# Stationary tiles with 16 or 32 bytes between their rows, in a two-layer decoder trunk on one core

## The chip, the cores and the metric

The kernel runs on one core of a Trainium2 chip. The metric is the device time of one execution in microseconds (us), lower is better; before the change it is 2203.47 us, the median of two runs (2203.27 to 2203.67).

## What is computed

A trunk of two layers over 256 tokens of width 2048, all in float32. Layer 0 mixes tokens by spatial gating and a sparse attention, layer 1 by a short convolution; both end in a gated feed-forward of width 5632. Cut to what matters here, the products with the large weights:

```python
def trunk(x):                                   # x [256, 2048]
    h = x
    h = h + mixer0(rmsnorm(h) @ w_in_ab) @ w_out_ab    # [2048, 4632], [2048, 2048]
    h = h + swiglu(rmsnorm(h), w_gate[0], w_up[0], w_down[0])
    b, c, z = split(rmsnorm(h) @ w_in_c, 3)             # [2048, 6144]
    h = h + (b * conv3(c * z)) @ w_out_c                # [2048, 2048]
    h = h + swiglu(rmsnorm(h), w_gate[1], w_up[1], w_down[1])
    return rmsnorm(h)

def swiglu(h, w_gate, w_up, w_down):            # [2048, 5632] x2, [5632, 2048]
    return (silu(h @ w_gate) * (h @ w_up)) @ w_down
```

## The kernel before

Every product is computed by the class `Stream`. A weight is read once, in blocks of 512 columns, and a block in loads of four K tiles (128 rows each) into one of three `raw` tiles. Two K tiles are a unit. `split` makes two fp32r parts of a unit's weights: ScalarE writes the high part `wh` (L82), VectorE the rest `wl` (L83). `multiply` then issues, for each K tile and each of the two token tiles, three matmuls that add up in one PSUM bank: high activations by high weights (L99), high by low (L100), low by high (L101). In all of them the activations are the stationary operand, 128 x 128 values that a weight load (LDWEIGHTS in the profile, engine row PEld) puts into the array, and 512 columns of weights are the moving one. `run` keeps the split three units ahead of the products, and calls hooks between units, in which the rest of the work stands (transposes, attention, evictions).

The activations that are stationary are kept as pairs of tiles, high and low, with one row of S = 256 values for each K tile: `a_h` and `a_l` (16 K tiles, the normed input of every first product), `t_h` and `t_l` (44 K tiles, the hidden layer of the feed-forward, source of `w_down`), `z_h` and `z_l` (16, the convolution's result, source of `w_out_c`), and `y0` and `y1` (16, the mixer's result, source of `w_out_ab`; the profile calls both y). They are written by `split_T`: transposes on TensorE into a PSUM bank (L223), then ScalarE writes the high part (L234, L239) and VectorE the low one (L235, L241), two K tiles at once in L234 and L235. y's attention half is written at L615 and L616 instead.

A K tile's row is 256 x 4 = 1024 bytes, and the second token tile starts 512 bytes into it. So every stationary operand of a tile starts at the same place modulo 512 bytes. The moving tiles have rows of 2048 bytes, and their starts also agree modulo 512.

Two more groups of products use fp32r: the gate's (L496, stationary 48 columns from an `xv` tile with rows 192 bytes apart, moving 256 columns of a_h or a_l) and the compressed blocks' (L398, stationary 60 columns from an earlier y tile with rows 240 bytes apart, moving 128 columns of weights).

`rest_loads` (L203) loads gains and encodings into two small constant tiles, `rows` and `pes`, with six DMAs from ScalarE's queue; `rest_T` transposes them (L213, L214). The pool `tok` has two buffers of 4096 bytes a partition, used in turn by tiles called `tk`, among them the two of L379, in which the windows of the compression are built.

Of the kernel before, what the change touches and what calls it, by code (L numbers as in the profile page):

```python
# [8 lines left out]
F32 = mybir.dt.float32  # L9
# [6 lines left out]
P = 128  # L16
S = 256
# [10 lines left out]
NEG = -1e30  # L28
AHEAD = 3
PROBS, VALUES = 4, 6  # L30


class Stream:
    """Weight tiles in the order of their use: loaded, split into two 12-bit parts, multiplied."""

    def __init__(self, nc, raws, parts, psg):
        self.nc, self.raws, self.parts, self.psg = nc, raws, parts, psg
# [4 lines left out]
        self.at_unit = 0  # L42

    def gemm(self, w, groups, n0, src, done, tail=0, between=None):
        """One column block of a product: K tiles in groups of four, or (first, number), two of them a unit. In the last `tail` units the
        first token tile goes before the second. `between` has units to put between the groups."""
        chunk = {"ps": None, "done": done}
        for gi, g in enumerate(groups):
            k0, gk = g if isinstance(g, tuple) else (g, 4)
            ri = len(self.raw_plan)  # L50
            self.raw_plan.append((w[k0 * P:(k0 + gk) * P, n0:n0 + NW].rearrange("(k p) n -> p k n", p=P), gk * NW))
            for j in range(gk // 2):
                self.units.append({
                    "raw": ri, "j": j, "k0": k0 + 2 * j, "src": src, "chunk": chunk, "free": j == gk // 2 - 1,
                    "first": gi == 0 and j == 0, "last": gi == len(groups) - 1 and j == gk // 2 - 1, "tail": 0,
                })
            if between and gi < len(groups) - 1:
                ap, use = between.pop(0)
                self.units.append({"raw": len(self.raw_plan), "j": 0, "use": use, "free": True})
                self.raw_plan.append((ap, 2 * NW))  # L60
        if tail:
            self.units[-tail]["tail"] = tail
# [86 lines left out]
def trunk(ctx: ExitStack, tc: tile.TileContext, x, norm_mix, norm_ffn, norm_f, w_in_ab, w_out_ab, sgu_w, sgu_b,  # L149
# [14 lines left out]

    st = Stream(nc, raws, parts, psg)

    # ---- residual stream, gains, constants
    h = acts.tile([P, MT, D], F32, name="h")
    a_h = acts.tile([P, KT, S], F32R, name="a_h")
    a_l = acts.tile([P, KT, S], F32R, name="a_l")  # L170

    row0 = const.tile([16, P], F32, name="row0")
    rows = const.tile([104, P], F32, name="rows")
    pes = const.tile([64, P], F32, name="pes")
    xt = x[0].rearrange("(m p) d -> p m d", p=P)

    def x_load(eng, c):
# [5 lines left out]
    nc.gpsimd.memset(mhalf, -0.5)  # L183

    def fold(n):
        """[2n, n]: two identities, one below the other"""
        t = const.tile([2 * n, n], F32, name=f"fold{n}")
        nc.gpsimd.memset(t, 0.0)
        for base in (0, -n):
            nc.gpsimd.affine_select(out=t, in_=t, compare_op=ALU.not_equal, fill=1.0, base=base, pattern=[[-1, n]],  # L190
                                    channel_multiplier=1)
        return t
# [8 lines left out]
    g_sgub = gains[:, 112:120]  # L201

    def rest_loads():  # L203
        nc.scalar.dma_start(out=rows[0:16], in_=norm_mix[1].rearrange("(k p) -> k p", p=P))
        nc.scalar.dma_start(out=rows[16:48], in_=norm_ffn.rearrange("l (k p) -> (l k) p", p=P))
        nc.scalar.dma_start(out=rows[48:96], in_=conv_w.rearrange("o j (k p) -> (o j k) p", p=P))
        nc.scalar.dma_start(out=rows[96:104], in_=sgu_b[0])
        nc.scalar.dma_start(out=pes[0:32], in_=cmp_pe_k[0])
        nc.scalar.dma_start(out=pes[32:64], in_=cmp_pe_v[0])

    def rest_T():
        t = bank()
        nc.tensor.transpose(t[:, :104], rows, ident[:104, :104])  # L213
        nc.tensor.transpose(t[:, 104:168], pes, ident[:64, :64])  # L214
        nc.vector.tensor_copy(gains[:, 16:], t[:, :104])
        nc.vector.tensor_copy(peT, t[:, 104:168])

    def transposed_bank(src, c):
        """A bank [P, 2, S]: the transpose of two 128-column tiles of src [P, MT, *] from column c."""
        t = bank()  # L220
        for k in range(2):
            for m in range(MT):
                nc.tensor.transpose(t[:, k * S + m * P:k * S + (m + 1) * P], src[:, m, c + k * P:c + (k + 1) * P], ident)  # L223
        return t.rearrange("p (k s) -> p k s", s=S)
# [21 lines left out]
        nc.scalar.activation(j, src, AF.Square, accum_out=into)  # L246

    def rsqrt_mean(ss, n, width, name, r=None):
        """1 / sqrt(ss / n + eps) of ss [P, width]"""
        v = small.tile([P, width], F32, name="v_" + name)  # L250
        nc.vector.tensor_scalar(v, ss, 1.0 / n, EPS, op0=ALU.mult, op1=ALU.add)
        if r is None:
            r = const.tile([P, width], F32, name="r_" + name)
        nc.gpsimd.tensor_tensor(r, v, mhalf[:, :width], op=ALU.pow)
        return r
# [6 lines left out]
    R = {}  # L262

    def norm_from(name, gain, after=None):
        """A callback for the column blocks of a product that adds to h and feeds the next norm."""
        ssp = const.tile([P, MT, 4], F32, name="ssp_" + name)

        def block(c):
            def done(ps):
                for m in range(MT):  # L270
                    hs = h[:, m, c * NW:(c + 1) * NW]
                    nc.vector.tensor_add(hs, ps[m], hs)
                    square_sum(hs, ssp[:, m, c:c + 1])

                def later():
                    split_T(transposed(h, c * NW), (a_h, a_l), 4 * c, gain)
                    if c == 3:
                        R[name] = row_scale(ssp, name)
                        if after:
                            after()  # L280

                st.at(1, later)

            return done

        return block

    # ---- layer 0: projections, gated spatial mixing, sparse attention
    stage = ExitStack()

    def region(name, bufs=1):
# [22 lines left out]
    def x_tiles(b):  # L314
        split_T([transposed_bank(h, b * S)], (a_h, a_l), 2 * b, g_mix[0])

    # masks and biases of the attention
    NC = 15
    dist, cbias, cmask = [], [], []

# [48 lines left out]
    def done_cmp(ps):  # L369
        x_scale()  # L370
        t = []

        def later(i):
            """The windows of 32 rows, with their encodings, as [d, row, part, group, window]."""
            w = tok.tile([P, MT * NW], F32, name="tk")[:, :64 * NC].rearrange("p (l g c) -> p l g c", l=32, g=2)
            v = transposed_bank(t[0], i * S).rearrange("p g (c l) -> p l g c", l=16)
            for j in range(2):
                pe = peT[:, i * 32 + 16 * j:i * 32 + 16 * j + 16]
                nc.vector.tensor_add(w[:, 16 * j:16 * j + 16], v[:, :, :, j:j + NC],  # L379
                                     pe[:, :, None, None].to_broadcast([P, 16, 2, NC]))  # L380
            xc[i] = yp.tile([P, 32, 2, 2 * NC], F32R, name=f"y{i}")
            w = w.rearrange("p l g c -> p l (g c)")
            nc.scalar.activation(xc[i][:, :, 0], w, AF.Copy)
            nc.vector.tensor_sub(xc[i][:, :, 1], w, xc[i][:, :, 0].bitcast(F32))

        st.at(1, lambda: t.append(to_tok(ps, r0)))
        st.at(2, lambda: later(0))
        st.at(3, lambda: later(1))
# [55 lines left out]
        nc.gpsimd.memset(t, 0.0)  # L444

    def cmp_out_v():
        """The compressed values, once for each head of a group: rows 32 r to 32 r + 14 for head r."""
        t = bank()
        for g in range(2):
            nc.tensor.matmul(t[:, g * P:(g + 1) * P], hgv[:, g].rearrange("p r n -> p (r n)"), w2[:, 1], start=True,  # L450
# [140 lines left out]
        nc.vector.tensor_mul(sm, sm, gv[:, :, 0])  # L591
        nc.vector.tensor_mul(s, s, sm[:, :, None].to_broadcast([P, 4, NC]))
    def compressed_T(g, qt):
        """The transposed probabilities of four heads, as the diagonal blocks of pcT."""
        t = bank()
        nc.tensor.transpose(t[:, :P], csp[(2 * g + qt) % 2].rearrange("p r n -> p (r n)"), ident)
        for r in range(4):
# [18 lines left out]
        nc.vector.tensor_sub(y_l[:, hs, qs], ov, y_h[:, hs, qs].bitcast(F32))  # L616

    def attention(first, step):
        """Background work between the units: each stage some units after the one that it waits for."""
        for g in range(2):  # L620
            for qt in range(MT):
                u = first + step * (8 * g + 4 * qt)
# [112 lines left out]
    for c in range(4):  # L735
        st.gemm(w_out_ab[0], [0, 8, 12, 4], c * NW, src_y, blk(c))

    # ---- feed-forward
    ff = {}

    def feed_forward(layer, rname, blk):
        src = [None, None]

        def done_gate_ff(c):
            def done(ps):
                if c == 0:
                    next_region()
                    big = region(f"big{layer}")
                    ff["tk"] = region(f"fft{layer}")
                    src[0] = big.tile([P, FKT, S], F32R, name="t_h")  # L750
                    src[1] = big.tile([P, FKT, S], F32R, name="t_l")
                t = ff["tk"].tile([P, MT, NW], F32, name="ga")
                for m in range(MT):
                    nc.scalar.activation(t[:, m], ps[m], AF.Silu, scale=R[rname][:, m:m + 1])
# [23 lines left out]

    feed_forward(0, "f0", norm_from("c1", g_mix[1]))

    # ---- layer 1: gated short convolution
    cv = {}
    wc = w_in_c[0]
    src_z = [None, None]
# [1 line left out]
    def done_cg(c):  # L786
        def done(ps):
            if c == 0:
                next_region()
                pool = region("conv")  # L790
                cv["p"] = region("convt", 2)
                src_z[0] = pool.tile([P, KT, S], F32R, name="z_h")
                src_z[1] = pool.tile([P, KT, S], F32R, name="z_l")
                r2 = const.tile([P, MT], F32, name="r2")
                nc.vector.tensor_mul(r2, R["c1"], R["c1"])
                cv["r2"] = r2
# [52 lines left out]
    for c in range(4):  # L849
        st.gemm(w_out_c[0], G4, c * NW, src_z, blk(c))  # L850

    # ---- last feed-forward and norm
    nf = {}
    ssf = const.tile([P, MT, 4], F32, name="ssp_o")

# [55 lines left out]
    g_ps = bank()  # L911

    def keep_warm(n):
        """Transposes of the identity, to nowhere, while the tensor engine has no data yet."""
        for _ in range(n):
            nc.tensor.transpose(g_ps[:, P:2 * P], ident, ident)

# [46 lines left out]
```

## Time and profile before

| what | value |
| --- | --- |
| median of the runs | 2203.47 us |
| span of the profiled execution, first to last instruction | 2201.5 us |
| time around the span (median less span) | 2.0 us |
| TensorE busy, matmul rows | 2190.7 us |
| weight loads (PEld) | 1797.6 us |
| VectorE busy | 1149.7 us |
| ScalarE busy | 988.1 us |
| mean granted TensorE clock | 0.999 |

The profile is of one execution. A matmul's row runs until its last result is out, so rows of matmuls that follow each other overlap, and their mean length is more than the time from one start to the next; the latter is read from the timeline, whose first column is the start and second the length. In the chain of waits, pieces are cut where the next begins, so that `x8` beside 0.94 us is eight steps in that time. Rows of groups give busy time and the mean of one in ns, then the idle time before them.

### The profile page before, as it was taken

The page shows a single profiled execution, that of the slowest core. Times are in us where ns is not written, and L with a number is a line of the kernel's source. Part 1 is how long each engine was busy: PE and PEld are TensorE (multiplying, and loading weights), DVE is VectorE, ACT ScalarE, POOL GpSimd, SP SyncE. Part 2 cuts the span into 40 slices and gives each one's busy share as a digit, 9 for nine tenths or more (in the row PEclk, how much of TensorE's full clock was granted, in tenths as well). Part 3 has the DMA queues.
Part 4 walks back from the last instruction along what each step waited for, and adds up shares of the span by engine and source line. Part 5 has one row for each costly group of instructions (what it writes and reads, how often), then busy time and mean ns, then how long its engine had stood idle before and what let it go on. Part 6 is the DMA issues. An engine that isn't in the chain of part 4 may idle for free.

```text
span 2201.5 us, 24410 instructions
## 1 busy us (share of the span) xinstructions
PE 2190.7 (100%) x9900; PEld 1797.6 (82%) x9900; DVE 1149.7 (52%) x1269; ACT 988.1 (45%) x1178; POOL 28.6 (1%) x59
## 2 busy tenths in 40 slices
PE   9999999999999999999999999999999999999998
PEld 7887788888888888888888888888888888888886
DVE  6577655455445544444455555554544455444444
ACT  6456545444444444444444444444444444434443
POOL 2000000000000000000000000000000000000000
PEclk9999999999999999999999999999999999999999
DMA  8654455656655555555556555556655655555553
GB/s 261 207 190 134 135 184 179 191 191 191 191 191 190 182 190 185 190 188 180 187 186 197 191 184 179 191 188 193 188 188 190 191 191 191 191 187 191 191 189 133
DMA packets 214577, 410.95 MB, mean 187 GB/s; under 512 B 6744, under 2 KB 18448, under 8 KB 214464
## 3 DMA queue, kind: packets, MB, share of 16 engines
q1 hardware_dynamic: 210416, 404.52, 56.7%
q10 hardware_dynamic: 3664, 3.63, 0.5%
q8 instruction: 77, 1.26, 0.2%
q0 software_dynamic: 384, 1.25, 0.2%
q14 instruction: 36, 0.29, 0.0%
HBM read 407.27 MB, written 2.10 MB: 186 GB/s over the span
## 4 chain that ended last, share of the span: by engine, by line
PE 99%; issue 0%; DMA 0%; DVE 0%; SPq 0%; POOLq 0%; POOL 0%; ACT 0%; DVEq 0%
PE pg L99 32%; PE pg L101 32%; PE pg L100 32%; PE pm L223 2%; PE pm L532 0%; PE pm L609 0%; PE pm L398 0%; PE pm L565 0%; DMA h<-in_x_dram 0%; PE pm L496 0%; PE pm L683 0%; PE pm L612 0%; PE pm L572 0%; POOLq L959 0%; POOL nf_r L892 0%
## 5 line engine op out<-in xcount | busy, mean ns | idle before, releaser
L83 DVE TENSOR_TENSOR wl<-raw,wh 128x1024 fp32r<-128x1024 f32 (+1 forms) x769 | 939.3, 1224 | 937.1 <-ACT wh L82 933.4
L82 ACT ACTIVATE wh<-raw 128x1024 fp32r<-128x1024 f32 (+1 forms) x769 | 811.8, 1058 | 976.7 <-PE pg L101 967.2
L99 PE MATMUL pg<-wh,a_h 128*128 128x512 f32 x2080 | 820.2, 394 | 0.0
L101 PE MATMUL pg<-wh,a_l 128*128 128x512 f32 x2080 | 810.4, 390 | 0.0
L100 PE MATMUL pg<-wl,a_h 128*128 128x512 f32 x2080 | 809.9, 389 | 0.0
L99 PEld LDWEIGHTS pg<-wh,a_h 128*128 128x128 f32 x2080 | 390.9, 188 | 81.5 <-issue 2.2
L100 PEld LDWEIGHTS pg<-wl,a_h 128*128 128x128 f32 x2080 | 390.9, 188 | 81.4 <-issue 2.2
L101 PEld LDWEIGHTS pg<-wh,a_l 128*128 128x128 f32 x2080 | 390.6, 188 | 81.8
L99 PE MATMUL pg<-wh,t_h 128*128 128x512 f32 x704 | 278.2, 395 | 0.0
L101 PE MATMUL pg<-wh,t_l 128*128 128x512 f32 x704 | 277.8, 395 | 0.0
L100 PE MATMUL pg<-wl,t_h 128*128 128x512 f32 x704 | 277.8, 395 | 0.0
L99 PEld LDWEIGHTS pg<-wh,t_h 128*128 128x128 f32 x704 | 132.6, 188 | 31.0
L101 PEld LDWEIGHTS pg<-wh,t_l 128*128 128x128 f32 x704 | 132.6, 188 | 31.0
L100 PEld LDWEIGHTS pg<-wl,t_h 128*128 128x128 f32 x704 | 132.6, 188 | 30.8
L99 PE MATMUL pg<-wh,y 128*128 128x512 f32 x128 | 51.0, 398 | 0.0
L99 PE MATMUL pg<-wh,z_h 128*128 128x512 f32 x128 | 50.8, 397 | 0.0
L100 PE MATMUL pg<-wl,z_h 128*128 128x512 f32 x128 | 50.5, 395 | 0.0
L101 PE MATMUL pg<-wh,z_l 128*128 128x512 f32 x128 | 50.5, 395 | 0.0
L101 PE MATMUL pg<-wh,y 128*128 128x512 f32 x128 | 50.4, 394 | 0.0
L100 PE MATMUL pg<-wl,y 128*128 128x512 f32 x128 | 50.4, 394 | 0.0
L235 DVE TENSOR_TENSOR t_l<-pm,t_h 128x512 fp32r<-128x512 f32 x44 | 28.4, 686 | 32.5 <-ACT t_h L234 32.5
L234 ACT ACTIVATE t_h<-pm 128x512 fp32r<-128x512 f32 x44 | 23.9, 597 | 46.3 <-PE pm L223 46.3
(182 smaller groups left out, 780.1 us busy)
## 6 DMA issues: line engine op xcount, KB each, us to landing
raw<-in_w_gate_dram SPq DMA_DIRECT2D x88, 1024.0 KB, 5.1
raw<-in_w_up_dram SPq DMA_DIRECT2D x88, 1024.0 KB, 5.2
raw<-in_w_down_dram SPq DMA_DIRECT2D x88, 1024.0 KB, 5.1
raw<-in_w_in_c_dram SPq DMA_DIRECT2D x48, 1024.0 KB, 5.1
raw<-in_w_in_ab_dram SPq DMA_DIRECT2D x34, 1024.0 KB, 5.2
raw<-in_w_out_ab_dram SPq DMA_DIRECT2D x16, 1024.0 KB, 5.1
raw<-in_w_out_c_dram SPq DMA_DIRECT2D x16, 1024.0 KB, 5.1
raw<-in_w_in_ab_dram SPq DMA_DIRECT2D x4, 512.0 KB, 6.6
```

What stands on the lines that cost most here:

```text
L82: nc.scalar.activation(hv[:, ks], src[:, ks], AF.Copy)
L83: nc.vector.tensor_sub(lv[:, ks], src[:, ks], hv[:, ks].bitcast(F32))
L99: nc.tensor.matmul(ps[m], xh[:, kt, sl], hv[:, k, :], start=u["first"] and k == 0, stop=False)
L100: nc.tensor.matmul(ps[m], xh[:, kt, sl], lv[:, k, :], start=False, stop=False)
L101: nc.tensor.matmul(ps[m], xl[:, kt, sl], hv[:, k, :], start=False, stop=u["last"] and k == 1)
L223: nc.tensor.transpose(t[:, k * S + m * P:k * S + (m + 1) * P], src[:, m, c + k * P:c + (k + 1) * P], ident)
L234: nc.scalar.activation(dh[:, k0:k0 + 2, :], t, AF.Copy)
L235: nc.vector.tensor_sub(dl[:, k0:k0 + 2, :], t, dh[:, k0:k0 + 2, :].bitcast(F32))
```

## The change

The tiles a_h, a_l, z_h and z_l get rows of S + 8 values, t_h and t_l of S + 4, of which the first S are used as before; y keeps its rows. `rows` and `pes` are no longer tiles of their own (512 bytes a partition each), but slices of a `tk` tile. The rest of the diff takes out comments.

```diff
+PAD, FPAD = 8, 4
...
-    a_h = acts.tile([P, KT, S], F32R, name="a_h")
-    a_l = acts.tile([P, KT, S], F32R, name="a_l")
+    a_h = acts.tile([P, KT, S + PAD], F32R, name="a_h")[:, :, :S]
+    a_l = acts.tile([P, KT, S + PAD], F32R, name="a_l")[:, :, :S]
...
-    rows = const.tile([104, P], F32, name="rows")
-    pes = const.tile([64, P], F32, name="pes")
...
     def rest_loads():
+        t = tok.tile([P, MT, NW], F32, name="tk")
+        rows, pes = t[:104, 0, :P], t[:64, 1, :P]
+        rest.extend((rows, pes))
...
+    rest = []
+
     def rest_T():
+        rows, pes = rest
...
-                    src[0] = big.tile([P, FKT, S], F32R, name="t_h")
-                    src[1] = big.tile([P, FKT, S], F32R, name="t_l")
+                    src[0] = big.tile([P, FKT, S + FPAD], F32R, name="t_h")[:, :, :S]
+                    src[1] = big.tile([P, FKT, S + FPAD], F32R, name="t_l")[:, :, :S]
...
-                src_z[0] = pool.tile([P, KT, S], F32R, name="z_h")
-                src_z[1] = pool.tile([P, KT, S], F32R, name="z_l")
+                src_z[0] = pool.tile([P, KT, S + PAD], F32R, name="z_h")[:, :, :S]
+                src_z[1] = pool.tile([P, KT, S + PAD], F32R, name="z_l")[:, :, :S]
```

On each engine the built program has the same instructions in the same order as before; only the shape that L234 and L235 write for t changes, from 128x512 to 128x2x256. The places in the partition, from the memory maps of the two programs (start in bytes, and that modulo 512):

| tile | start before | mod 512 | row before | start after | mod 512 | row after |
| --- | --- | --- | --- | --- | --- | --- |
| wh, first buffer (moving) | 44,672 | 128 | 2048 | 43,648 | 128 | 2048 |
| wl, first buffer (moving) | 61,056 | 128 | 2048 | 60,032 | 128 | 2048 |
| a_h | 93,824 | 128 | 1024 | 92,800 | 128 | 1056 |
| a_l | 110,208 | 128 | 1024 | 109,696 | 128 | 1056 |
| t_h | 129,024 | 0 | 1024 | 129,024 | 0 | 1040 |
| t_l | 174,080 | 0 | 1024 | 174,784 | 192 | 1040 |
| z_h | 129,024 | 0 | 1024 | 129,024 | 0 | 1056 |
| z_l | 145,408 | 0 | 1024 | 145,920 | 0 | 1056 |
| y0 | 163,776 | 448 | 1024 | 163,776 | 448 | 1024 |
| y1 | 180,160 | 448 | 1024 | 180,160 | 448 | 1024 |

## Rows read from the trace of the kernel before

**Rows 1.** The page, part 1: busy us (share of the span) x instructions

```profile
span 2201.5 us, 24410 instructions
PE 2190.7 (100%) x9900; PEld 1797.6 (82%) x9900; DVE 1149.7 (52%) x1269; ACT 988.1 (45%) x1178; POOL 28.6 (1%) x59
```

**Rows 2.** The page, part 4: the chain that ended last, by engine and line

```profile
PE 99%; issue 0%; DMA 0%; DVE 0%; SPq 0%; POOLq 0%; POOL 0%; ACT 0%; DVEq 0%
PE pg L99 32%; PE pg L101 32%; PE pg L100 32%; PE pm L223 2%; PE pm L532 0%; PE pm L609 0%; PE pm L398 0%; PE pm L565 0%; DMA h<-in_x_dram 0%; PE pm L496 0%; PE pm L683 0%; PE pm L612 0%; PE pm L572 0%; POOLq L959 0%; POOL nf_r L892 0%
```

**Rows 3.** Windows by stage (mostly y, a, t, z as stationary operand)

```profile
core 0: us, PE busy (x) PEld busy (x) DVE busy (x) ACT busy (x) POOL busy (x), PEclk, DMA share, GB/s
...
260.00:362.00 102.00, 102.00 (x456) 82.05 (x456) 54.30 (x61) 49.64 (x68) 0.00 (x0) 1.00 0.52 169
362.00:852.00 490.00, 490.00 (x2210) 406.66 (x2209) 246.22 (x226) 214.04 (x226) 1.61 (x1) 1.00 0.59 189
852.00:1101.00 249.00, 249.00 (x1089) 202.00 (x1088) 118.55 (x111) 103.90 (x120) 0.00 (x0) 1.00 0.56 185
...
1365.00:1462.00 97.00, 97.00 (x441) 79.13 (x440) 52.90 (x58) 47.37 (x68) 0.00 (x0) 1.00 0.54 179
1462.00:1951.00 489.00, 489.00 (x2203) 405.75 (x2202) 245.49 (x226) 211.97 (x223) 2.71 (x3) 1.00 0.60 191
```

**Rows 4.** Groups: matmuls of each stationary tile, and a weight load

```profile
L99 PE MATMUL pg<-wh,a_h 128*128 128x512 f32 x2080 | 820.2, 394 | 0.0
...
L99 PEld LDWEIGHTS pg<-wh,a_h 128*128 128x128 f32 x2080 | 390.9, 188 | 81.5 <-issue 2.2
...
L99 PE MATMUL pg<-wh,t_h 128*128 128x512 f32 x704 | 278.2, 395 | 0.0
...
L99 PE MATMUL pg<-wh,y 128*128 128x512 f32 x128 | 51.0, 398 | 0.0
L99 PE MATMUL pg<-wh,z_h 128*128 128x512 f32 x128 | 50.8, 397 | 0.0
```

**Rows 5.** Timeline of TensorE, products with a_h and a_l, 15 rows

```profile
499.69 0.39 PE L99 MATMUL pg<-wh,a_h 128*128 128x512 f32 x1
...
502.87 0.39 PE L101 MATMUL pg<-wh,a_l 128*128 128x512 f32 x1
```

**Rows 6.** Timeline of TensorE, products with y, 12 rows

```profile
349.83 0.39 PE L100 MATMUL pg<-wl,y 128*128 128x512 f32 x1
...
352.40 0.39 PE L99 MATMUL pg<-wh,y 128*128 128x512 f32 x1
```

**Rows 7.** Timeline of TensorE, products with t_h and t_l, 18 rows

```profile
1001.02 0.39 PE L100 MATMUL pg<-wl,t_h 128*128 128x512 f32 x1
...
1003.35 0.40 PE L101 MATMUL pg<-wh,t_l 128*128 128x512 f32 x1
1003.59 0.39 PE L99 MATMUL pg<-wh,t_h 128*128 128x512 f32 x1
...
1004.98 0.40 PE L99 MATMUL pg<-wh,t_h 128*128 128x512 f32 x1
```

**Rows 8.** Timeline of TensorE, products with z_h and z_l, 15 rows

```profile
1419.62 0.40 PE L101 MATMUL pg<-wh,z_l 128*128 128x512 f32 x1
...
1422.88 0.40 PE L100 MATMUL pg<-wl,z_h 128*128 128x512 f32 x1
```

**Rows 9.** The chain of waits in time: gate, compressed blocks, transposes, plain products

```profile
63.82 0.94 PE pm L496 x8
64.76 0.96 PE pm L398 x16
...
145.04 0.87 PE pm L223 x8
165.81 1.72 PE pm L609 x4
```

**Rows 10.** Loads and transposes of rows and pes, next writes of tk

```profile
21.89 0.34 ACTq L204 DMA_DIRECT2D rows<-in_norm_mix_dram  x1
...
24.98 0.43 ACTq L209 DMA_DIRECT2D pes<-in_cmp_pe_v_dram  x1
...
L213 PE MATMUL pm<-ident,rows x1: 253/253/253, 33.6 to 33.6; 104*128 104x104 f32 x1
...
L379 DVE TENSOR_TENSOR tk<-pm,peT x4: 642/646/657, 40.2 to 46.0; 128x480 f32<-128x480 f32 x4
```

**Rows 11.** Groups: evictions that write t and y

```profile
L235 DVE TENSOR_TENSOR t_l<-pm,t_h 128x512 fp32r<-128x512 f32 x44 | 28.4, 686 | 32.5 <-ACT t_h L234 32.5
L234 ACT ACTIVATE t_h<-pm 128x512 fp32r<-128x512 f32 x44 | 23.9, 597 | 46.3 <-PE pm L223 46.3
...
L616 DVE TENSOR_TENSOR y<-pm,y 128x512 fp32r<-128x512 f32 x4 | 2.8, 692 | 13.8 <-ACT y L615 13.8
L615 ACT ACTIVATE y<-pm 128x512 fp32r<-128x512 f32 x4 | 2.4, 597 | 20.2 <-PE pm L612 20.2
```

**Rows 12.** Loads and matmuls of L496 and L398: ns min/median/max

```profile
L398 PEld LDWEIGHTS pm<-wh,y x64: 129/132/136, 64.5 to 127.6; 128*60 128x60 f32 x64
...
L496 PEld LDWEIGHTS pm<-a_h,xv x16: 121/121/123, 59.3 to 69.8; 128*48 128x48 f32 x16
L496 PE MATMUL pm<-a_h,xv x16: 276/279/281, 59.5 to 69.9; 128*48 128x256 f32 x16
```

## The prediction

> **What bounds the kernel now.** I read the totals first, then the chain of waits, then the stages, then single rows. The totals say that TensorE is busy 2190.7 of 2201.5 us, VectorE 52% and ScalarE 45% [rows 1]. The chain that ended last is 99% TensorE, and nearly all of that is three lines, the three products of `multiply` (L99 to L101), with 32% each [rows 2]. In the stage windows TensorE is busy without a hole, the granted clock is 1.00 (the 2.4 GHz level), and the DMA share is 0.52 to 0.60 [rows 3]. So the time is a number of matmuls times the step from the start of one to the start of the next, and only a change of that step can move it by much. There are 2080 x 3 = 6240 of the large matmuls on a_h and a_l, 704 x 3 = 2112 on t_h and t_l, 384 on z and 384 on y [rows 4]; the mean in that view is the length of one, whose end overlaps the next, so the step has to be read from the start times.
>
> The timeline gives it. On a_h/a_l 14 steps take 502.87 - 499.69 = 3.18 us, 227.1 ns each [rows 5]. On y 11 steps take 2.57 us, 233.6 each [rows 6]. On t_h/t_l 17 steps take 3.96 us, 232.9 each, and they are uneven (1003.35 to 1003.59 is 240) [rows 7]. On z 14 steps take 3.26 us, 232.9 [rows 8]. All four have the same shapes, the same moving tiles and an unbroken queue. What differs is where the stationary tile lies: the moving tiles start at 128 modulo 512, and so do a_h and a_l; t and z lie at 0, y at 448 (table of addresses above). The cheapest step belongs to the tile at the same place as the moving one.
>
> How short could the step be? Plain float32 matmuls show the floor: eight transposes of 128 columns take 0.87 us, 109 ns each, and four products of 512 columns 1.72 us, 430 each [rows 9]. That is (430 - 109) / 384 = 0.836 ns a column and 2.0 ns a matmul. The fp32r products take 227.1 ns or more for 512 columns, so they read faster than that; I estimate half, 0.418 ns (one column a cycle at the 2.4 GHz level), which makes 512 x 0.418 + 2.0 = 216.0 ns. So a loses 11.1 ns in a step, t and z 16.9, y 17.6. The weight load of the next matmul runs during each step (188 ns for 128 columns [rows 4]), and a loss that depends on the stationary tile's place points to the reads of that load and of the moving tile getting in each other's way.
>
> **The change, part by part.** No instruction is added, removed or moved on any engine. Three things change.
>
> (1) The place for rows and pes. The six small loads now write a tile of the pool tok, and the third user of that pool waits for them and for their transposes. They are issued at 21.9 to 25.0 us and the two transposes run at 33.6 us; the first write that can meet them, L379, is at 40.2 us [rows 10]. Cost nothing; the cover is some 6 us.
>
> (2) The written shape. Two K tiles of t_h were one run of 512 values, and are now two of 256 with a gap. The row to go by is y, already written in four separate pieces of 128: 597 ns on ScalarE and 692 on VectorE, against 597 and 686 for t_h [rows 11]. So 44 x 6 ns on VectorE, 0.3 us, on an engine that is idle half of the time: nothing. If the cover were gone it would cost these 0.3 us.
>
> (3) The places of the stationary rows. a and z now walk by 32 bytes a K tile through all 16 multiples of 32, t by 16 bytes through 32 places; t_l starts 192 further than t_h. y stays at 448. So the steps of 6240 + 2112 + 384 = 8736 matmuls become a mean over places, of which the trace shows three for this shape: 227.1, 232.9 and 233.6.
>
> Two small groups of fp32r matmuls already walk through places. The gate's products (L496, stationary rows 192 bytes apart, eight places) take 0.94 us for 8, 117.5 ns; the floor for 256 columns is 109.0, so each loses 8.5 ns. The compressed blocks' products (L398, rows 240 bytes apart) take 0.96 us for 16, 60.0 ns; the floor for 128 columns is 55.5, a loss of 4.5 [rows 9]. Their loads are shorter: 121 ns for 48 columns and 132 for 60, against 188 for 128 [rows 12], which is (188 - 121) / 80 = 0.84 ns a column, so that the reading itself lasts about 40, 50 and 107 ns. If the loss goes with the time of reading, a walked load of 128 columns loses 4.5 x 107 / 50 = 9.6 to 8.5 x 107 / 40 = 22.7 ns, and the step is 225.6 to 238.7. These are my bounds; the middle is 232.2. I take the middle of the places seen for the shape itself, (227.1 + 233.6) / 2 = 230.4, since they are the nearest rows.
>
> The sum: a, 6240 x (230.4 - 227.1) = +20.6 us; t, 2112 x (230.4 - 232.9) = -5.3; z, 384 x -2.5 = -1.0. Together +14.3 us. The profiled span is 2201.5 us, the runs' median 2203.5, so 2.0 us lie around the span and stay: 2203.5 + 14.3 = 2217.8 us. At the bounds: 225.6 gives 6240 x -1.5 - 2496 x 7.3 = -27.6 us, 2176; 238.7 gives 6240 x 11.6 + 2496 x 5.8 = +86.9 us, 2290. The step at which nothing changes is (6240 x 227.1 + 2496 x 232.9) / 8736 = 228.8 ns; 2%, about what a measurement of this kernel can tell from no change, is 44.1 us or 5.05 ns a step.
>
> **Rivals.** *The spread gets the loss out of the way (faster).* Three places of 32 are seen, and the other ones may be cheaper than 227.1: at 220.0 ns the gain is 8736 x 8.8 = 76 us, 2127; at the floor of 216.0 it is 111 us, 2092. It is over 2% below 223.7 ns. For it: the step does depend on the place. Against it: the gate's matmuls go through eight places, and their lengths are 276 to 281 ns [rows 12], so none of the eight is free of the loss. The Trainium skill (TensorE: Matmul & The Clock Gate, "Wait — 56ns, not 53.3ns?") gives the start-to-start step as the columns at the full clock plus about 2.5 ns, an estimate of 215.8 ns here; by that rule this rival would be worth its whole price, and the trace of before disagrees with it, with 227.1 at best.
>
> *The spread takes a_h off its good place (slower).* The tile with most matmuls is at the cheapest place seen. If the others cost what y and t cost, the step is 233.6: 6240 x 6.5 + 2496 x 0.7 = +42 us, 2246. It passes +2% above 233.8 ns, and at the gate's rate it reaches 2290. For it: two of three places are dear, and the gate's loss for each column loaded is twice that of a_h. Against it: the compressed blocks' products lose less than a_h for each column (4.5 / 60 against 11.1 / 128 ns).
>
> *The place modulo 512 does nothing, and the change doesn't do what it says (same).* a_h and a_l lie below byte 126,592 of the partition, t, z and y above 129,024, so another property of the address could make the difference. Then 2203.5 stays. The Trainium skill (SBUF — State Buffer, "Who interferes with whom") says that TensorE has one read port for the moving operand and an independent one for the weight load, and never waits on anyone; by it no place could matter, and the sum is zero. The trace speaks against it with 227.1 against 233.6 ns for the same work, though it doesn't prove which property of the place decides.
>
> **How the numbers follow.** A mixture of places with a step between 223.7 and 233.8: 0.42, with its own range of 2176 to 2247. No effect of the place: 0.14. Faster by the first rival: 0.22. Slower by the second: 0.22. So faster 0.22, same 0.56, slower 0.22. The range runs from 2135 (a step of 220.9, half of the first rival's chance left out below) to 2262 (235.5, less than half of the second's left out above).
>
> **What would show it.** Right: in the profile after, the steps on a_h/a_l differ from one K tile to the next with a mean near 230, those on t and z have a mean near 230, those on y stay at 233.6, weight loads stay near 188 ns, and ScalarE's t_h rows stay near 597. Wrong: a step on a that is even at 227 although its rows walk (the place does nothing), a mean under 224 or over 234 (the rivals), or y moving too, which would mean that something other than its place sets it. If TensorE became so fast that it waited for wh or raw, the DMA share of 0.52 to 0.60 says that this would need far more than the floor gives.

## The result: slower by 1.5%, and the profile after

The changed kernel takes 2236.34 us (2236.30 to 2236.38), against 2203.47 before: a ratio of 1.0149, 95% interval 1.012 to 1.0179, or +32.9 us. The forecast was +14.3 us: the right sign, inside the range, and less than half of the size.

The totals after (lines of the kernel are further down: L99 to L101 of `multiply` are now L100 to L102, L234 and L235 of `split_T` are L239 and L240):

```profile
span 2234.6 us, 24413 instructions
## 1 busy us (share of the span) xinstructions
PE 2222.7 (99%) x9900; PEld 1796.5 (80%) x9900; DVE 1149.2 (51%) x1269; ACT 988.0 (44%) x1178; POOL 27.3 (1%) x59
...
PE 99%; DMA 0%; issue 0%; DVE 0%; ACT 0%; SPq 0%; POOLq 0%; POOL 0%; DVEq 0%; ACTq 0%
...
L100 PE MATMUL pg<-wh,a_h 128*128 128x512 f32 x2080 | 832.7, 400 | 0.0
L102 PE MATMUL pg<-wh,a_l 128*128 128x512 f32 x2080 | 821.5, 395 | 0.0
L101 PE MATMUL pg<-wl,a_h 128*128 128x512 f32 x2080 | 819.0, 394 | 0.7 <-DVE wl L84 0.7
...
L101 PEld LDWEIGHTS pg<-wl,a_h 128*128 128x128 f32 x2080 | 391.1, 188 | 93.5 <-issue 2.2
...
L100 PE MATMUL pg<-wh,t_h 128*128 128x512 f32 x704 | 278.1, 395 | 0.0
...
L240 DVE TENSOR_TENSOR t_l<-pm,t_h 128x512 fp32r<-128x512 f32 x44 | 28.4, 686 | 33.7 <-ACT t_h L239 33.7
L239 ACT ACTIVATE t_h<-pm 128x512 fp32r<-128x512 f32 x44 | 23.9, 595 | 47.5 <-PE pm L228 47.5
```

Nothing but TensorE's time has moved: the chain is TensorE's as before [rows 2], the other engines are busy as long, a weight load takes 188 ns as in [rows 4], and the evictions of t, for all their new shape, take 595 and 686 ns as in [rows 11]. The matmuls on a_h are 6 ns longer (400 after 394), those on t_h are not (395).

The stretches of the timeline that answer to [rows 5], [rows 6] and [rows 7] (31, 15 and 19 rows; start, length):

```profile
503.88 0.39 PE L100 MATMUL pg<-wh,a_h 128*128 128x512 f32 x1
504.10 0.39 PE L101 MATMUL pg<-wl,a_h 128*128 128x512 f32 x1
...
505.74 0.40 PE L102 MATMUL pg<-wh,a_l 128*128 128x512 f32 x1
505.98 0.40 PE L100 MATMUL pg<-wh,a_h 128*128 128x512 f32 x1
...
510.86 0.40 PE L100 MATMUL pg<-wh,a_h 128*128 128x512 f32 x1
...
354.70 0.39 PE L101 MATMUL pg<-wl,y 128*128 128x512 f32 x1
...
357.97 0.39 PE L100 MATMUL pg<-wh,y 128*128 128x512 f32 x1
...
1019.67 0.39 PE L101 MATMUL pg<-wl,t_h 128*128 128x512 f32 x1
...
1023.83 0.39 PE L101 MATMUL pg<-wl,t_h 128*128 128x512 f32 x1
```

On a, 30 steps take 510.86 - 503.88 = 6.98 us, 232.7 ns each, after an even 227.1. In the trace's nanoseconds the single steps of this stretch go from 226 to 241; those of [rows 5] were 226 or 227. On y it is 3.27 us for 14 steps, 233.6 as before. On t, 4.16 us for 18 steps, 231.1 after 232.9. Over all matmuls in the whole trace that follow one on the same tiles, waits included, the mean step on a went from 228.8 to 234.5 ns, on t from 232.7 to 231.9, and stayed at 233.4 on z and at 234.7 to 234.8 on y. In us that is 6240 x 5.7 - 2112 x 0.8 = 35.6 - 1.7 = +33.9, against +32.9 measured. So the whole loss is on a_h and a_l.

In the same trace the steps on a can be sorted by the place of the tile that is being loaded, as its distance from the moving tile's place (bytes modulo 512; steps of 260 ns and more, which hold a wait, left out). Means in ns:

| distance | 0 | 32 | 64 | 96 | 128 | 160 | 192 | 224 |
| --- | --- | --- | --- | --- | --- | --- | --- | --- |
| a, walking | 231.2 | 233.3 | 233.4 | 232.9 | 232.9 | 233.3 | 230.9 | 233.4 |
| the same + 256 | 231.4 | 233.3 | 233.1 | 232.9 | 232.9 | 233.3 | 230.9 | 233.3 |

Two things stand out: distances that differ by 256 agree within 0.3 ns, and even at distance 0 a no longer has its 227. It doesn't settle there either: a K tile has six steps, and the five between two of its own matmuls take 230.9 ns on the average at distances 0 and 256.

### The profile page after: what moved, and what is told of

Read it like the earlier page. It is cut to its first block, busy times and chain, and to the rows that moved or that the text cites. A ratio compares the mean times of both kernels' runs of the same rounds, so it can differ in the third digit from the quotient of the medians.

```text
span 2234.6 us, 24413 instructions
## 1 busy us (share of the span) xinstructions
PE 2222.7 (99%) x9900; PEld 1796.5 (80%) x9900; DVE 1149.2 (51%) x1269; ACT 988.0 (44%) x1178; POOL 27.3 (1%) x59
## 4 chain that ended last, share of the span: by engine, by line
PE 99%; DMA 0%; issue 0%; DVE 0%; ACT 0%; SPq 0%; POOLq 0%; POOL 0%; DVEq 0%; ACTq 0%
PE pg L100 32%; PE pg L102 32%; PE pg L101 31%; PE pm L228 2%; PE pm L537 0%; PE pm L614 0%; PE pm L403 0%; DMA raw<-in_w_in_ab_dram 0%; PE pm L570 0%; PE pm L501 0%; PE pm L688 0%; PE pm L617 0%; PE pm L577 0%; DVE wl L84 0%; POOLq L964 0%
## 5 line engine op out<-in xcount | busy, mean ns | idle before, releaser
L100 PE MATMUL pg<-wh,a_h 128*128 128x512 f32 x2080 | 832.7, 400 | 0.0
L102 PE MATMUL pg<-wh,a_l 128*128 128x512 f32 x2080 | 821.5, 395 | 0.0
L101 PE MATMUL pg<-wl,a_h 128*128 128x512 f32 x2080 | 819.0, 394 | 0.7 <-DVE wl L84 0.7
L102 PEld LDWEIGHTS pg<-wh,a_l 128*128 128x128 f32 x2080 | 390.3, 188 | 94.8
L101 PEld LDWEIGHTS pg<-wl,a_h 128*128 128x128 f32 x2080 | 391.1, 188 | 93.5 <-issue 2.2
L100 PEld LDWEIGHTS pg<-wh,a_h 128*128 128x128 f32 x2080 | 391.1, 188 | 90.8 <-issue 2.2
L100 PE MATMUL pg<-wh,t_h 128*128 128x512 f32 x704 | 278.1, 395 | 0.0
L101 PE MATMUL pg<-wl,t_h 128*128 128x512 f32 x704 | 277.4, 394 | 0.0
L102 PE MATMUL pg<-wh,t_l 128*128 128x512 f32 x704 | 276.6, 393 | 0.0
L102 PEld LDWEIGHTS pg<-wh,t_l 128*128 128x128 f32 x704 | 132.2, 188 | 31.3
L100 PEld LDWEIGHTS pg<-wh,t_h 128*128 128x128 f32 x704 | 132.3, 188 | 30.9
L101 PEld LDWEIGHTS pg<-wl,t_h 128*128 128x128 f32 x704 | 132.3, 188 | 30.0
L100 PE MATMUL pg<-wh,y 128*128 128x512 f32 x128 | 51.0, 399 | 0.0
L100 PE MATMUL pg<-wh,z_h 128*128 128x512 f32 x128 | 50.9, 398 | 0.0
L102 PE MATMUL pg<-wh,z_l 128*128 128x512 f32 x128 | 50.5, 395 | 0.0
L101 PE MATMUL pg<-wl,y 128*128 128x512 f32 x128 | 50.5, 394 | 0.0
L102 PE MATMUL pg<-wh,y 128*128 128x512 f32 x128 | 50.5, 394 | 0.0
L101 PE MATMUL pg<-wl,z_h 128*128 128x512 f32 x128 | 50.4, 394 | 0.0
L240 DVE TENSOR_TENSOR t_l<-pm,t_h 128x512 fp32r<-128x512 f32 x44 | 28.4, 686 | 33.7 <-ACT t_h L239 33.7
L239 ACT ACTIVATE t_h<-pm 128x512 fp32r<-128x512 f32 x44 | 23.9, 595 | 47.5 <-PE pm L228 47.5
```

The lines of the kernel that those rows point to most:

```text
L100: nc.tensor.matmul(ps[m], xh[:, kt, sl], hv[:, k, :], start=u["first"] and k == 0, stop=False)
L101: nc.tensor.matmul(ps[m], xh[:, kt, sl], lv[:, k, :], start=False, stop=False)
L102: nc.tensor.matmul(ps[m], xl[:, kt, sl], hv[:, k, :], start=False, stop=u["last"] and k == 1)
L239: nc.scalar.activation(dh[:, k0:k0 + 2, :], t, AF.Copy)
L240: nc.vector.tensor_sub(dl[:, k0:k0 + 2, :], t, dh[:, k0:k0 + 2, :].bitcast(F32))
```

## Experiments: which part costs the time

Theory A: what gave a its 227 ns is that all its loads are at the same place as the moving tiles; a walk takes that away. Theory B: a differs from t, z and y by the part of the partition it lies in, not by its place modulo 512. Theory C: the place of rows and pes, or the shift of what lies behind them, costs the time. All kernels below are the changed one with edits; the two constants for the rows become three, for a, t and z. Without longer rows the tiles start 1024 bytes lower than before at most, at the same places modulo 512.

**e1, longer rows on a alone.**

```diff
-PAD, FPAD = 8, 4
+APAD, TPAD, ZPAD = 8, 0, 0
```

> The change with the longer rows on a_h and a_l alone; t and z keep rows of 1024 bytes. In the profile after, the mean step rose by 5.7 ns on a (228.8 to 234.5, waits included) and fell by 0.8 on t. Theory A (a constant place, the same as the moving tiles', is what gave a its 227 ns; walking rows lose it): a alone carries the loss, 6240 x 5.7 = +35.5 us, 2239 us, t back at 232.7 to 232.9. Theory C (the move of rows and pes, or the shift of everything behind them, costs the time): +33 us as well, but then the run with all rows unpadded is slow too.

Measured: 2237.96 us, ratio 1.0157 (1.0144 to 1.0171). a alone carries the loss, 1.6 us more than the whole change, in which t gained 1.7.

**e2, longer rows on t and z alone.**

```diff
-PAD, FPAD = 8, 4
+APAD, TPAD, ZPAD = 0, 4, 8
```

> The change with the longer rows on t and z alone. Theory A: a is back at 227 ns, t gains 2112 x 0.8 = 1.7 us: 2202 us, no difference that can be measured. If a longer row by itself costs (whatever the place), t and z would lose too, as they do not in the profile after; then this run would stay above 2205.

Measured: 2201.62 us, ratio 0.9992 (0.9983 to 1.0001), no difference that can be told from none; by the medians -1.7 us, which is what t's step gives. On a 15 steps take 3.40 us, 226.7 ns:

```profile
499.70 0.39 PE L100 MATMUL pg<-wh,a_h 128*128 128x512 f32 x1
...
503.10 0.39 PE L100 MATMUL pg<-wh,a_h 128*128 128x512 f32 x1
```

**e3, no longer row at all.**

```diff
-PAD, FPAD = 8, 4
+APAD, TPAD, ZPAD = 0, 0, 0
```

> The change without any longer row: only rows and pes lie in the pool tok, and all tiles behind them start 1024 bytes lower, at the same places modulo 512. Theory A: 2203.5 us and the steps of before (227 on a, 232.9 on t and z, 233.5 on y). Theory C: 2236 us.

Measured: 2203.46 us, ratio 1.0 (0.9991 to 1.0009). Theory C falls; the cover of the loads of rows and pes [rows 10] held.

**e4, everything at one place.** Rows as in e3; small unused tiles ahead of t, z and y bring them to a's place.

```diff
+                    big.tile([P, 32], F32, name="gap_t")
                     src[0] = big.tile([P, FKT, S + TPAD], F32R, name="t_h")[:, :, :S]
...
+                pool.tile([P, 32], F32, name="gap_z")
                 src_z[0] = pool.tile([P, KT, S + ZPAD], F32R, name="z_h")[:, :, :S]
...
+    mix.tile([P, 48], F32, name="gap_y")
     sw = mix.tile([P, 8, P], F32, name="sw")
```

> No longer rows; t, z and y start 128, 128 and 192 bytes later, so that all of them lie at 128 modulo 512 like a and the moving tiles. Theory A (the place relative to the moving tile): t, z and y fall to 227 ns, 2112 x 5.8 + 384 x 5.9 + 384 x 6.5 = 17.0 us less, 2186.5 us. Theory B (the difference between a and t, z, y comes from the part of the partition in which they lie, above or below byte 127,000, not from the place modulo 512): nothing changes, 2203.5 us.

Measured: 2187.96 us, ratio 0.993 (0.9917 to 0.9942): 15.4 us faster than before, 48 faster than the change. The timelines of t (19 rows) and of y (15 rows) in it:

```profile
984.82 0.39 PE L101 MATMUL pg<-wl,t_h 128*128 128x512 f32 x1
...
988.90 0.39 PE L101 MATMUL pg<-wl,t_h 128*128 128x512 f32 x1
...
344.67 0.39 PE L102 MATMUL pg<-wh,y 128*128 128x512 f32 x1
...
347.84 0.39 PE L101 MATMUL pg<-wl,y 128*128 128x512 f32 x1
```

18 steps in 4.08 us are 226.7 ns on t, 14 in 3.17 us are 226.4 on y. They lie in the same part of the partition as before, so theory B falls. Of the 17.0 us that were expected 15.4 came: a's own step is 229.1 with waits instead of 228.8.

## Experiments: which property of the place

**e5, the moving tiles are shifted**, and everything else keeps its place modulo 512.

```diff
-PAD, FPAD = 8, 4
+APAD, TPAD, ZPAD = 0, 0, 64
...
     parts = ctx.enter_context(tc.tile_pool(name="parts", bufs=AHEAD + 1))
+    parts.tile([P, 32], F32, name="gap_p", bufs=1)
...
+    acts.tile([P, 96], F32, name="gap_a")
     a_h = acts.tile([P, KT, S + APAD], F32R, name="a_h")[:, :, :S]
```

> No longer rows on a, t and y; the moving tiles wh and wl start 128 bytes later (256 modulo 512), while a, t, z and y keep their places modulo 512 (128, 0, 0, 448). z gets rows of 1280 bytes, so that its K tiles are in turn 256 and 0 bytes from the moving tiles' place. Relative theory (only the distance between stationary and moving place counts): a, now 128 bytes below the moving tiles, rises from 227 to 232.9 ns as t had it: 6240 x 5.8 = +36 us. Absolute theory (the place 128 modulo 512 is good in itself): a stays at 227. If distances that differ by 256 are equal (after the change a's means at such pairs agree, 231.2 and 231.4 at 0 and 256), t at 256 falls to 227: -12 us, 2227 us together, and z, though its place changes with each K tile, has 227 too; if not, t keeps about 233 (2239 us) and z is uneven.

Measured: 2222.63 us in one run, 18.7 more than the run of before beside it. (From here on each kernel ran once; the argument rests on the steps inside its trace.) a and t have changed places, though neither moved modulo 512:

```profile
504.66 0.40 PE L101 MATMUL pg<-wl,a_h 128*128 128x512 f32 x1
...
508.17 0.39 PE L101 MATMUL pg<-wl,a_h 128*128 128x512 f32 x1
...
1009.65 0.39 PE L101 MATMUL pg<-wl,t_h 128*128 128x512 f32 x1
...
1013.95 0.39 PE L102 MATMUL pg<-wh,t_l 128*128 128x512 f32 x1
```

15 steps in 3.51 us are 234.0 on a (mean of the trace 232.8), 19 in 4.30 us are 226.3 on t (mean 226.7), which is 256 bytes from the moving place. On z, whose K tiles are in turn 256 and 0 bytes away, the means are 227.0 and 226.8. So it is the distance between the stationary and the moving operand that counts, modulo 256. And a walk in steps of 256 bytes costs nothing: it is not the change of place in itself, nor the longer row.

**s1, s2 and s3, other constant distances**, made with unused tiles ahead, as in e4 (s3: with slices that begin 16 bytes into the tile). In s1, for a:

```diff
+    acts.tile([P, 56], F32, name="gap_a")
     a_h = acts.tile([P, KT, S + APAD], F32R, name="a_h")[:, :, :S]
```

> No longer rows; constant places at other distances from the moving tiles: a 224, t 192, z 32, y 96 bytes. Theory A says that a constant place at another distance than 0 (or 256) costs between 227 and 236 ns, with no row below 224 on the average: a at 233 gives 2240 us. If some distance is cheaper than 0, its mean step is under 226 and a better kernel than all so far lies there.

> No longer rows on a, t and y; constant distances: a 96, t 160, y 288 bytes (32 above 256). z lies at distance 0 with rows of 1536 bytes, longer but at the same place modulo 512. Theory A: a, t and y between 227 and 236 ns; z at 227 in spite of the longer rows. If the length of the row counts, z is above 230.

> No longer rows; constant distances that are odd multiples of 16: a 16, t 240, z 48, y stays at 320. So far, modulo 256: 226.8 at 0, 229.0 at 192, and 232.6 to 234.3 at 32, 64, 96, 128, 160 and 224. If the step depends on the distance in a smooth way around 0, 16 and 240 lie between 227 and 233 (a at 230: +19 us); if 0 is a single cheap place, they are at 233 (+37 us). A step under 226 would be a better place than any so far.

Measured in one run each: s1 2234.86, s2 2247.25, s3 2211.63 us. Mean steps over the stage in the trace (those of 260 ns and more left out), by the distance modulo 256, from all runs with constant places (which tile in brackets):

| distance | mean step, ns |
| --- | --- |
| 0 | 227.0 (a), 226.7 (t), 227.0 (y), 226.9 (z), and 226.8 (z, rows of 1536 bytes) |
| 16 | 229.9 (a), a mean of 226.7 and 233.3, see below |
| 32 | 233.3 (z), 233.3 (y) |
| 48 | 233.3 (z) |
| 64 | 233.3 (y) |
| 96 | 234.2 (a), 234.3 (y) |
| 128 | 232.5 (t), 232.6 (z), 232.8 (a) |
| 160 | 233.3 (t) |
| 192 | 228.9 (t), 229.0 (y) |
| 224 | 233.3 (a) |
| 240 | 227.1 (t) |

For example, in s2 a at 96 bytes (16 rows), in s1 t at 192 (19 rows) and in s3 t at 240 (20 rows):

```profile
504.62 0.40 PE L101 MATMUL pg<-wl,a_h 128*128 128x512 f32 x1
...
508.14 0.40 PE L101 MATMUL pg<-wl,a_h 128*128 128x512 f32 x1
```

```profile
1014.71 0.39 PE L100 MATMUL pg<-wh,t_h 128*128 128x512 f32 x1
...
1018.83 0.39 PE L100 MATMUL pg<-wh,t_h 128*128 128x512 f32 x1
```

```profile
1003.65 0.39 PE L101 MATMUL pg<-wl,t_h 128*128 128x512 f32 x1
...
1007.96 0.39 PE L102 MATMUL pg<-wh,t_l 128*128 128x512 f32 x1
```

These are 234.7, 228.9 and 226.8 ns a step. Different tiles at the same distance agree within 0.4 ns. The good places, 0 with 240 beside it and 192, are the exception: of the eight multiples of 32, six cost 232.5 to 234.3, and their mean over all eight is (226.9 + 233.3 + 233.3 + 234.2 + 232.6 + 233.3 + 228.9 + 233.3) / 8 = 232.0. The walk of the change has 232.7 over its 16 places: within 0.7 ns it takes the mean of the constant places, though not place by place, since its own 16 means lie between 230.9 and 233.4. None of the eleven places tried, of sixteen multiples of 16, is cheaper than 0, so e4 stays the best version.

The mean at 16 hides two levels. In s3 the unbroken stretches of 40 and more steps on a take 226.7 ns (18 of 31) or 233.3 to 233.4 (13). In the first feed-forward the two alternate, stretch by stretch, with eight transposes between them. Two pieces of 31 rows, from one stretch and the next:

```profile
429.13 0.39 PE L100 MATMUL pg<-wh,a_h 128*128 128x512 f32 x1
...
435.93 0.39 PE L100 MATMUL pg<-wh,a_h 128*128 128x512 f32 x1
...
470.51 0.39 PE L100 MATMUL pg<-wh,a_h 128*128 128x512 f32 x1
...
477.51 0.39 PE L100 MATMUL pg<-wh,a_h 128*128 128x512 f32 x1
```

The 30 steps take 6.80 and 7.00 us, 226.7 and 233.3 ns each, on the same tiles at the same places. So the distance is not the whole condition: something else, which lasts through a stretch and which no run here isolates, decides between the levels. At distance 0 no such stretch in any of the runs with 128 loaded columns is above 227.2.

## Experiments: where the loss of each matmul comes from

The prediction held that the loss over the floor of 216 ns is made by the reading of the weight load. Three runs take pieces of the work away.

**e6, half of the stationary columns** (rows as in e3), and **e7, 8 of them** (`n = 8`).

```diff
+            whole = u["first"] and k == 0 or u["last"] and k == 1
+            n = P if whole else P // 2
             for m in ms:
-                sl = slice(m * P, (m + 1) * P)
-                nc.tensor.matmul(ps[m], xh[:, kt, sl], hv[:, k, :], start=u["first"] and k == 0, stop=False)
+                sl = slice(m * P, m * P + n)
+                o = ps[m][:n]
+                nc.tensor.matmul(o, xh[:, kt, sl], hv[:, k, :], start=u["first"] and k == 0, stop=False)
...
```

> No longer rows, places as before; in all large products but those of the first and last K tile of a block only 64 of the 128 stationary columns are loaded and multiplied (half of the sums is left out). The moving operand still has 512 columns. If the loss comes from the weight load's reading, it falls with it: half of 11.1, 16.9 and 17.6 ns, so about 221.5 on a, 224.5 on t and z, 224.8 on y; together about 50 us less, 2153. If the loss is a fixed price of a new matmul, or of reading at full rate, nothing changes: 2203.5.

Measured: 2213.64 us in one run, 9.7 more than before. t's mean step fell by 2.0, to 230.5, and a's rose by 2.6, to 229.6. Neither reading in the expectation came: the loss was not halved, and the steps did not stay.

> As the run with half loads, but only 8 of the 128 stationary columns are loaded (15 of 16 sums are left out, except for the first and last K tile of a block). Halving the load took 2 ns from t and added 2.6 to a, against the expectation. Theory L (the loss is made by the weight load's reading): with 1/16 of the load next to nothing is left of it, 216 to 219 ns everywhere, about 2105 us. Theory M (the loss goes with the moving operand's 512 columns: 4.5 ns at 128, 8.5 at 256 and 14 to 17 at 512 are 0.033 ns a column, whatever is loaded): 228 to 233 ns on all tiles, 2200 to 2230 us.

Measured: 2205.92 us in one run, 2.7 more than before. The group of a_l's loads (busy us, mean ns), and 13 steps of t in the timeline:

```profile
L105 PEld LDWEIGHTS pg<-wh,a_l 128*8 128x8 f32 x1820 | 159.7, 88 | 254.8 <-issue 0.2
```

```profile
1000.81 0.39 PE L105 MATMUL pg<-wh,t_l 128*8 128x512 f32 x1
...
1003.82 0.40 PE L103 MATMUL pg<-wh,t_h 128*8 128x512 f32 x1
```

The load takes 88 ns instead of 188, and the step on t is still 3.01 us / 13 = 231.5 ns (mean of the trace 231.5; a 228.0, y 231.6, z 231.7). Theory L falls.

**e8, half of the moving columns on z**, with a full load.

```diff
+            whole = u["first"] and k == 0 or u["last"] and k == 1 or u["src"] is not src_box[0]
+            n, w = (P, NW) if whole else (P, NW // 2)
...
+                o = ps[m][:n, :w]
+                nc.tensor.matmul(o, xh[:, kt, sl], hv[:, k, :w], start=u["first"] and k == 0, stop=False)
...
```

> Places as before; in the products with z alone the moving operand has 256 of its 512 columns (half of the sums is left out, except for the first and last K tile of a block), while all 128 stationary columns are loaded. Read from the steps inside a unit, since the weights' loads can't follow at twice the pace. Theory L: the loss of 16.9 ns stays, 109 + 17 = 126 ns a step. Theory M: half of it, 8.5: 117.5 ns, as in the gate's products, which load 48 columns.

Measured: 2175.38 us in one run. In an unbroken stretch of 35 rows on z:

```profile
1399.98 0.28 PE L108 MATMUL pg<-wh,z_l 128*128 128x256 f32 x1
...
1404.02 0.28 PE L106 MATMUL pg<-wh,z_h 128*128 128x256 f32 x1
```

34 steps in 4.04 us are 118.8 ns, 9.8 over the floor of 109.0: near theory M's 117.5 and far from theory L's 126. All sizes side by side, over the prediction's floor:

| moving columns | loaded columns | step, ns | over 0.418 a column + 2.0 | a moving column |
| --- | --- | --- | --- | --- |
| 128 | 60 (L398) | 60.0 | 4.5 | 0.035 |
| 256 | 48 (L496) | 117.5 | 8.5 | 0.033 |
| 256 | 128 (e8, z) | 118.8 | 9.8 | 0.038 |
| 512 | 8 (e7, t) | 231.5 | 15.5 | 0.030 |
| 512 | 64 (e6, t) | 230.5 | 14.5 | 0.028 |
| 512 | 128 (before, t) | 232.5 | 16.5 | 0.032 |

The loss goes with the columns that stream (0.028 to 0.038 ns a column), not with those that are loaded. The distance then decides how much of it is spared: some 6 to 7 ns of 17 at the best place with 128 loaded columns (226.8 against 232.5 to 234.3).

## Why the prediction came out as it did

*That TensorE's step sets the time, and that parts (1) and (2) of the change cost nothing: right.* e3 has the move of rows and pes alone at a ratio of 1.0 (0.9991 to 1.0009), and the evictions of t took 595 and 686 ns.

*That a sits at its cheapest place, and that the distance to the moving tile is the cause: right,* as e4 and e5 show, though it counts modulo 256 and not 512, and at 16 it doesn't decide alone. The third rival, that the place does nothing, falls with them. The Trainium skill (SBUF — State Buffer, "Who interferes with whom") has TensorE wait on nobody, with separate read ports for its two operands. Where that is read as in the prediction, so that no place can matter, the runs disagree: with nothing but the distance changed, the step on t goes from 232.5 to 226.7 ns. The measurement decides.

*The step that failed: "I take the middle of the places seen for the shape itself, (227.1 + 233.6) / 2 = 230.4".* Three places had been seen, two dear and one cheap, and a middle between the ends counts the one as heavily as all others. Measured, the cheap place is the exception; the mean is 232.0 over the eight constant places and 232.7 on a's walk. So the term for a, +20.6 us, should have been +35.6, the term for t, -5.3, was -1.7, and that for z, -1.0, was nothing. The plain mean of the three steps seen, 231.2, would have been nearer. It would still have been too low, since it gives distance 0 its 227 within the walk, and there the trace shows 231.2.

*The bounds rested on a wrong reason.* That "the loss goes with the time of reading" was worked out from two small groups that differ in both operands. Their moving columns, 128 and 256, explain their 4.5 and 8.5 ns at one stroke (0.035 and 0.033 a column), and at 512 would have given 17 to 18 ns, a step of 233 to 234: close to what came. The rows were on the table; the wrong one of two sizes was scaled. With e7 the reason itself falls: with a sixteenth of the columns to load, t still takes 231.5 ns. That the middle of these bounds, 232.2, lies within 0.5 ns of a's 232.7 is luck. The floor of 216.0 below all of this is an estimate that no fp32r row here reaches.

*The rivals.* The slower one ("The spread takes a_h off its good place") named what happened: its price, 2246 us at a step of 233.6 everywhere, is 10 us above the result. The faster one falls: no place tried is cheaper than the one that a had. What was held against it, that none of the gate's eight places is free of the loss, pointed the right way. Its floor is reached nowhere in these runs: the lowest mean step is 226.7. The Trainium skill (TensorE: Matmul & The Clock Gate, "Wait — 56ns, not 53.3ns?") would put it at 215.8, an estimate; for these fp32r operands of 512 columns no run here comes nearer than 226.7.

*What could be told apart.* The prediction took 2% (44.1 us) for the limit. The loss of 32.9 us is below it, but the 21 runs of before beside e1 to e4 lie between 2203.03 and 2204.62 us, so a change of 1.5% is plain here.

*Open:* why fp32r products take about 0.03 ns more than the floor for each moving column (with no run at the floor, this may be a loss or simply their rate), how the stationary operand's place acts on that, and what chooses between the two levels at 16. With 8 columns loaded a (228.0) is still cheaper than t (231.5), so a short load is enough for the place to act; with 64 the gap is down to 0.9 (229.6 against 230.5). That the reads of the two operands get in each other's way was only argued; no run here shows it.

## What to carry to other kernels

Where a kernel is a chain of equal matmuls, read the step from successive starts and sort it by operand: a difference of 3% between operands of equal shape can be the address, which costs next to nothing to change. Bring all operands to the good distance and keep them there (here the stationary tile at the moving tile's place modulo 256: 15 us from three unused tiles of 128 to 192 bytes) instead of spreading them, since the spread bought about the mean here. And when two small groups are scaled up to a large one, write down every size in which they differ before choosing which one to scale.

## What was not expected

- The place acts modulo 256 bytes, not 512: rows of 1280 bytes, which go from one half to the other with each K tile, keep 226.8 and 227.0 ns.
- A second good distance at 192 (228.9 and 229.0 ns on two tiles), between dear ones at 160 and 224 (233.3).
- A load of 8 columns instead of 128 leaves the step of a full fp32r matmul within 1 ns on t (231.5 after 232.5), and the load still takes 88 ns.
- At distance 0 the step is 226.7 to 227.0 where the place is constant, and 231.2 in the walk, where only six matmuls in a row share a place.
- At distance 16 the same tiles run whole stretches at 226.7 ns and others at 233.3.
